# An encoder kernel with 64 sets of matmuls that nobody reads, set between the last norm and the output

## The chip, the cores and the metric

The kernel runs on one core of one Trainium2 chip. The metric is the device time of one execution in microseconds, taken on the chip. A profile is one execution recorded by the hardware profiler: its span goes from the first instruction to the end of the last one, and the engines in it are TensorE (PE, with its weight loads shown apart as PEld), VectorE (DVE), ScalarE (ACT), GpSimd (POOL) and SyncE (SP, which issues the DMAs here).

## The reference

A two-layer bidirectional encoder on 256 tokens of width 2048, all in float32. Each layer norms its input, projects it, runs a differential attention and a latent attention, merges the two through gates, adds the result to x, adds a SwiGLU and adds a gated embedding. At the end stands a norm:

```python
def rmsnorm(x, g, eps=NORM_EPS):
    xf = x.astype(jnp.float32)
    y = xf * lax.rsqrt(jnp.mean(xf * xf, axis=-1, keepdims=True) + eps)
    return (y * g.astype(jnp.float32)).astype(x.dtype)
...
        x = x + sigmoid(rmsnorm(x, g_ple[i]) @ w_ple_gate[i]) * e
    return rmsnorm(x, g_final)
```

## The kernel before

Everything is kept transposed: 128 channels on the partitions, 256 tokens along the row, 16 such blocks for the width of 2048. `xT` is the residual, one tile of 16 blocks.

**Matmuls in two parts.** A float32 number is split into a high part, which is a copy in the type fp32r, and a low part, which is the rest. For weights, `piece` (L168 on) loads up to 1024 columns into `w`, lets ScalarE copy them into a tile of the tag `whi` (L181) and VectorE write the rest into one of the tag `wlo`. Each of these two tags has three buffers, so a new tile takes the place of the one made three pieces ago and waits until the matmuls that read it are done. Activations are split into `ua` and `ub`, 16 tiles each with the high part in columns 0 to 255 and the low part in columns 256 to 511.

**Three kinds of matmul in fp32r.** In `emit`, for a usual product, a high block of weights is the stationary operand and a whole row of 512 columns (both parts of an activation) moves past it (L211), then the low block with the 256 high columns (L212). If `whole` is set, as for the last block of the kernel, there are three matmuls of 256 columns each (L207, L208, L209). In `values` (L392 to L394) it is the other way round: a block of 128 tokens of `ua` is stationary, and 512 columns of weights move.

**Norms.** `norm` sums squares over the partitions with matmuls that have a block of 128 columns in plain float32 as stationary operand and one column of `ones` moving (L271); on the chip each plain float32 matmul is two records in the profile. `rsqrt` is a string of small VectorE instructions. `spread` puts the result onto all partitions, by two multiplications with the identity (`dg`) and one plain float32 matmul of 256 columns (L280).

**The end.** In the last loop, for the 16 output blocks of `w_pg`, ScalarE joins the two parts of the product (L236), takes a sigmoid (L695), squares the new `xT` block (L263, L260) and scales it by the final gain (L683). Behind the loop stand the last `norm` and `spread`, whose result R stays in a bank of PSUM of the pool `ps_at`, which has two banks, and six multiplications of `xT` by R, each followed by its DMA to the output (L704).

**Order.** The program is written with a scheduler that places instructions on the engines and puts in the waits; each engine then runs its own list in order. An instruction that overwrites something waits for those that read it earlier in the program.

Of the kernel before, what the change touches and what calls it, by code (L numbers as in the profile page):

```python
# [13 lines left out]
F32R = mybir.dt.float32r  # L14
I32 = mybir.dt.int32
AF = mybir.ActivationFunctionType
# [3 lines left out]
P = 128  # L20
T = 256
# [15 lines left out]
PT = 8  # L37
# [15 lines left out]
def encoder(ctx, tc, x, p, positions, cols, lams, wq, wk, wv, wcq, wckv, wkr, wga, wgb,  # L53
            w_q_up, w_kn, w_v, w_bd, w_bm, w_out, w_gate, w_up, w_down, w_pin, w_pg, rope_c, out):
    nc = tc.nc
    V, A, PE = nc.vector, nc.scalar, nc.tensor
# [3 lines left out]
    wts = pool("wts")  # L60
    tmp = pool("tmp")
    stat = pool("stat")
    ps_mm = pool("ps_mm", 4, space=PSUM)
# [3 lines left out]
    def scratch(tag, bufs, n=T):  # L67
        return tmp.tile([P, n], F32, tag=tag, name=tag, bufs=bufs)

    def bank(ps=ps_at, tag="at", name="at", shape=(P, 2 * T)):  # L70
        return ps.tile(list(shape), F32, tag=tag, name=name)

    def tt(o, a, b, op):
        return V.tensor_tensor(out=o, in0=a, in1=b, op=op)  # L74
# [4 lines left out]
    def ts(o, a, s1, s2, op0, op1=ALU.bypass):  # L79
        return V.tensor_scalar(out=o, in0=a, scalar1=s1, scalar2=s2, op0=op0, op1=op1)  # L80


    ua = [const.tile([P, 2 * T], F32R, name=f"ua{j}") for j in range(NC)]
# [12 lines left out]
    xT = const.tile([P, NC, T], F32, name="xT")  # L96
# [4 lines left out]
    at = 0  # L101
# [10 lines left out]
    ones = const.tile([P, P], F32, name="ones")  # L112
# [2 lines left out]
    aside = [fa(j) for j in range(5)]  # L115
    posi = aside[0][:, 0, :].bitcast(I32)
    posf = aside[0][:, 1, :]

    def tables():
        V.tensor_copy(posf, posi)  # L120
        got = []
        for i, name in enumerate("pm"):
            ang, k, r, a = (aside[j + i][:, m, :] for j in (1, 3) for m in range(2))
            ts(ang, posf, rc[:, 2 * i : 2 * i + 1], None, ALU.mult)
            ts(k, ang, 1.0 / TWO_PI, ROUND, ALU.mult, ALU.add)
            ts(k, k, ROUND, None, ALU.subtract)
            stt(r, k, -C1, ang, ALU.mult, ALU.add)
            stt(r, k, -C2, r, ALU.mult, ALU.add)
            stt(r, k, -C3, r, ALU.mult, ALU.add)
            ts(r, r, PI_IN, -PI_IN, ALU.min, ALU.max)  # L130
            stt(a, r, -1.0, r, ALU.mult, ALU.min)
            ts(a, a, math.pi / 2, None, ALU.add)
            cs = const.tile([P, T], F32, name="cos_" + name)
            sn = const.tile([P, T], F32, name="sin_" + name)
            A.activation(cs, a, AF.Sin)
            A.activation(sn, r, AF.Sin)
            ts(sn, sn, rc[:, 2 * i + 1 : 2 * i + 2], None, ALU.mult)
            got += [cs, sn]
        return got
# [74 lines left out]
    def product(src, us, whole=False):  # L214


        acc = bank(ps_mm, "mm", "mm")
        n = len(us)
        for a in range(0, n, PT):
            m = min(PT, n - a)  # L220
            hi, lo = piece(src[:, a * P : (a + m) * P], m)
            emit(acc, hi, lo, 0, us[a : a + m], a == 0, a + m == n, whole)
        return acc[:, :T] if whole else acc
# [10 lines left out]
    def joined(acc, o=None):  # L234
        t = scratch("join", 3)
        A.activation(t, acc[:, T:], AF.Copy)  # L236
        o = scratch("a", 4) if o is None else o
        tt(o, acc[:, :T], t, ALU.add)
        return o
# [7 lines left out]
    def rsqrt(src, n, eps, width):  # L247

        v, y, a = (stat.tile([P, 2 * DH], F32, tag="r" + s, name="r" + s, bufs=2)[:, :width] for s in "vya")
        ts(v, src, 1.0 / n, eps, ALU.mult, ALU.add)  # L250
        ts(y.bitcast(I32), v.bitcast(I32), -0.5, 1597463007.0, ALU.mult, ALU.add)
        for _ in range(3):
            stt(a, y, -0.5, y, ALU.mult, ALU.mult)
            tt(a, a, v, ALU.mult)
            stt(y, a, 1.5, y, ALU.add, ALU.mult)
        return y

    def square_into(acc, src, first):
        if first:
            A.activation(acc, src, AF.Square)  # L260
        else:
            sq = scratch("sq", 2)
            A.activation(sq, src, AF.Square)  # L263
            tt(acc, acc, sq, ALU.add)

    def norm(sums, n):

        s = bank()
        for j, a in enumerate(sums):
            for b in range(2):  # L270
                PE.matmul(s[:, b : b + 1], a[:, b * P : (b + 1) * P], ones[:, 0:1], start=j + b == 0, stop=j + b == len(sums))  # L271
        return rsqrt(s[:, 0:2], n, EPS, 2)

    def spread(col, copied=True):

        dg = stat.tile([P, 2, P], F32, tag="dg", name="dg", bufs=1)
        for b in range(2):
            ts(dg[:, b, :], ident, col[:, b : b + 1], None, ALU.mult)
        s = bank()
        PE.matmul(s[:, :T], ones, dg, start=True, stop=True)  # L280
        if not copied:
            return s[:, :T]
        row = stat.tile([P, T], F32, tag="row", name="row", bufs=2)
        A.activation(row, s[:, :T], AF.Copy)  # L284
        return row

    def normed(sums, one, two):

        got = [joined(one())]
        col = norm(sums, DM)  # L290
        got.append(joined(two()))
        return spread(col), col, got

    def squares():
        return stat.tile([P, T], F32, tag="ssq", name="ssq", bufs=2)

    def stream(us, gain):

        acc = squares()

        def add(c):
            split(us[c], xT[:, c, :], g(gain, c))
            square_into(acc, xT[:, c, :], c == 0)

        return acc, add
# [110 lines left out]
    for L in range(DEPTH):  # L416

        steps = values(wv[L], ua, None if L else load)
        for vd in steps:
            if L == 0 and vd is not None:  # L420
# [3 lines left out]
                with after_splits():  # L424
                    rcol = norm([sq0[0][:, j, :] for j in range(2)], DM)
                    next(steps)
                    R = spread(rcol)
                    cos_p, sin_p, cos_m, sin_m = tables()
                    lambdas()
                break  # L430
            if L:
                next(steps)
                rcol = norm([acc], DM)
                next(steps)
                R = spread(rcol)
                break
# [5 lines left out]
        for o, t in ((cr, cos_p), (sr, sin_p), (crm, cos_m), (srm, sin_m)):  # L442
            tt(o, t, R, ALU.mult)

# [17 lines left out]
        def latent(us, w, raws):  # L462
            ss = squares()
            for c in range(len(us)):
                tt(raws[c], joined(product(w[L, c], ua)), R, ALU.mult)
                square_into(ss, raws[c], c == 0)
# [55 lines left out]
        def gate(w, store, n):  # L522
            tt(store(n), joined(product(w[L, n], ua)), R, ALU.mult)

# [115 lines left out]
        acc, add = stream(ub, f"g_ffn{L}")  # L640
# [4 lines left out]

        R, _, pre = normed([acc], lambda: product(w_gate[L, 0], ub), lambda: product(w_up[L, 0], ub))
        pT, es = ua[14:], []
# [4 lines left out]
        for part, (f0, f1) in enumerate(FF_PARTS):  # L652
            for f in range(f0, f1):
                a = pre.pop(0) if pre else joined(product(w_gate[L, f], ub))
# [5 lines left out]
                b = pre.pop(0) if pre else joined(product(w_up[L, f], ub))  # L660
# [3 lines left out]
            if last:  # L664
                acc, add = stream(ub, f"g_ple{L}")
# [10 lines left out]
        R, _, pre = normed([acc], lambda: product(w_pg[L, 0], ub), lambda: product(w_pg[L, 1], ub))  # L676
        final = L == DEPTH - 1
        if final:
            sums = [squares(), squares()]
# [5 lines left out]
        else:  # L685
            acc, add = stream(ua, f"g_mix{L + 1}")
        for n in range(NC):
            if final and n == NC - 1:
                a = scratch("a", 4)
                tt(a, product(w_pg[L, n], ub, True), R, ALU.mult)  # L690
            else:
                a = pre.pop(0) if pre else joined(product(w_pg[L, n], ub))
# [5 lines left out]
            add(n)  # L698

    R = spread(norm(sums, DM), copied=False)  # L700
    for n, m in ((0, 1), (1, 1), (2, 2), (4, 4), (8, 4), (12, 4)):
        o = xT[:, n : n + m, :]
        tt(o, o, R[:, None, :].to_broadcast([P, m, T]), ALU.mult)
        nc.sync.dma_start(out[:, n : n + m, :], o)  # L704
# [84 lines left out]
```

## Time and profile before

| | us |
|---|---|
| Median of 2 runs | 2867.84 |
| The two runs | 2866.69 and 2868.99 |
| The profiled execution | 2867.58 |
| Its span | 2865.8 |

The 1.78 us between the profiled execution's time and its span lie outside the recorded instructions. On the page, a row of a group of instructions gives the line, the engine, the operation, what is written and read (`out<-in`, moving operand first for a matmul), the shape and the count, then the busy time in us and the mean length of one in ns. A row of the timeline gives the start in us, the length in us, the engine, the line, the operation and how many were merged, and in brackets how long the engine had been idle and what ended that. Matmul lengths overlap: the time from one start to the next is what a matmul costs in a stream.

### The profile page before, as it was taken

The page shows a single profiled execution, that of the slowest core. Times are in us where ns is not written, and L with a number is a line of the kernel's source. Part 1 is how long each engine was busy: PE and PEld are TensorE (multiplying, and loading weights), DVE is VectorE, ACT ScalarE, POOL GpSimd, SP SyncE. Part 2 cuts the span into 40 slices and gives each one's busy share as a digit, 9 for nine tenths or more (in the row PEclk, how much of TensorE's full clock was granted, in tenths as well). Part 3 has the DMA queues.
Part 4 walks back from the last instruction along what each step waited for, and adds up shares of the span by engine and source line. Part 5 has one row for each costly group of instructions (what it writes and reads, how often), then busy time and mean ns, then how long its engine had stood idle before and what let it go on. Part 6 is the DMA issues. An engine that isn't in the chain of part 4 may idle for free.

```text
span 2865.8 us, 43980 instructions
## 1 busy us (share of the span) xinstructions
PE 2845.8 (99%) x16750; PEld 2507.7 (88%) x16750; DVE 2063.3 (72%) x3529; ACT 1524.2 (53%) x2529; POOL 1.7 (0%) x9
## 2 busy tenths in 40 slices
PE   9999999999999999999999999999999999999998
PEld 7888888888888888888888888888888888888887
DVE  7898658776666666677859976687766666666776
ACT  6676555554444444455646755555544444444554
POOL 0000000000000000000000000000000000000000
PEclk9999999999999999999999999999999999999999
DMA  7544566555665566566655445566556656655654
GB/s 233 171 162 148 162 193 199 192 191 187 184 199 194 182 198 201 194 193 191 189 188 166 154 154 168 193 197 194 188 188 185 198 194 187 200 194 194 193 190 140
DMA packets 156019, 532.40 MB, mean 186 GB/s; under 512 B 16928, under 2 KB 23840, under 8 KB 155808
## 3 DMA queue, kind: packets, MB, share of 16 engines
q1 hardware_dynamic: 155376, 529.01, 58.1%
q8 instruction: 131, 2.15, 0.3%
q14 instruction: 80, 0.66, 0.1%
q10 hardware_dynamic: 432, 0.59, 0.1%
HBM read 527.43 MB, written 2.10 MB: 185 GB/s over the span
## 4 chain that ended last, share of the span: by engine, by line
PE 98%; DVE 1%; ACT 0%; DMA 0%; issue 0%; SPq 0%; DVEq 0%
PE mm L211 61%; PE mm L212 31%; PE S L341 1%; PE mmv L394 1%; PE mmv L393 1%; PE mmv L392 1%; PE at L359 0%; PE at L563 0%; PE at L620 0%; DMA w<-in_wv 0%; DVE wlo L74 0%; DVE a L74 0%; PE at L280 0%; DVE xT L74 0%; ACT E L350 0%
## 5 line engine op out<-in xcount | busy, mean ns | idle before, releaser
L181 ACT ACTIVATE whi<-w 128x1024 fp32r<-128x1024 f32 (+2 forms) x1029 | 1067.0, 1037 | 1267.6 <-issue 722.6
L74 DVE TENSOR_TENSOR wlo<-w,whi 128x1024 fp32r<-128x1024 f32 (+2 forms) x1029 | 1229.6, 1195 | 703.8 <-ACT whi L181 694.7
L211 PE MATMUL mm<-ub,whi 128*128 128x512 f32 x3952 | 1360.8, 392 | 0.0
L211 PE MATMUL mm<-ua,whi 128*128 128x512 f32 x3744 | 1283.4, 390 | 0.0
L212 PE MATMUL mm<-ub,wlo 128*128 128x256 f32 x3952 | 1096.8, 278 | 0.0
L212 PE MATMUL mm<-ua,wlo 128*128 128x256 f32 x3744 | 1036.3, 277 | 0.0
L211 PEld LDWEIGHTS mm<-ub,whi 128*128 128x128 f32 x3952 | 741.9, 188 | 158.7
L211 PEld LDWEIGHTS mm<-ua,whi 128*128 128x128 f32 x3744 | 702.1, 188 | 143.9
L212 PEld LDWEIGHTS mm<-ub,wlo 128*128 128x128 f32 x3952 | 741.8, 188 | 0.8
L212 PEld LDWEIGHTS mm<-ua,wlo 128*128 128x128 f32 x3744 | 702.9, 188 | 2.3 <-DVE wlo L74 0.6
L74 DVE TENSOR_TENSOR a<-mm,join 128x256 f32<-128x256 f32 x421 | 175.7, 419 | 0.3 <-ACT join L236 0.2
L236 ACT ACTIVATE join<-mm 128x256 f32<-128x256 f32 x453 | 166.8, 369 | 5.0 <-PE mm L212 4.8
L74 DVE TENSOR_TENSOR xT<-xT,mm 128x256 f32<-128x256 f32 x256 | 106.9, 420 | 41.5 <-PE mm L212 37.7
L74 DVE TENSOR_TENSOR a<-a,row 128x256 f32<-128x256 f32 x207 | 87.4, 424 | 6.6 <-ACT row L284 0.8
L392 PE MATMUL mmv<-whi,ua 128*128 128x512 f32 x128 | 50.5, 396 | 3.8 <-ACT whi L181 3.8
L74 DVE TENSOR_TENSOR a<-a 128x256 f32<-128x256 f32 x120 | 51.0, 425 | 4.0
L74 DVE TENSOR_TENSOR ua<-a,ua 128x256 fp32r<-128x256 f32 x120 | 50.2, 418 | 1.0 <-ACT ua L244 1.0
L393 PE MATMUL mmv<-whi,ua 128*128 128x512 f32 x128 | 50.6, 396 | 0.0
L244 ACT ACTIVATE ua<-a 128x256 fp32r<-128x256 f32 x120 | 48.4, 403 | 2.7 <-DVE a L74 2.6
L350 ACT ACTIVATE E<-S,nm 128x256 f32<-128x256 f32 x96 | 44.3, 472 | 5.1 <-DVE nm L80 5.1
L394 PE MATMUL mmv<-wlo,ua 128*128 128x512 f32 x128 | 46.8, 397 | 0.1
L74 DVE TENSOR_TENSOR ssq<-ssq,sq 128x256 f32<-128x256 f32 x97 | 40.7, 420 | 0.5 <-ACT sq L263 0.5
(154 smaller groups left out, 1161.7 us busy)
## 6 DMA issues: line engine op xcount, KB each, us to landing
w<-in_w_gate SPq DMA_DIRECT2D x176, 512.0 KB, 4.7
w<-in_w_up SPq DMA_DIRECT2D x176, 512.0 KB, 4.7
w<-in_w_down SPq DMA_DIRECT2D x128, 512.0 KB, 4.2
w<-in_wga SPq DMA_DIRECT2D x64, 512.0 KB, 3.8
w<-in_wgb SPq DMA_DIRECT2D x64, 512.0 KB, 4.4
w<-in_w_out SPq DMA_DIRECT2D x64, 512.0 KB, 4.4
w<-in_w_pg SPq DMA_DIRECT2D x64, 512.0 KB, 4.7
w<-in_w_down SPq DMA_DIRECT2D x64, 384.0 KB, 3.7
```

Source lines behind the costliest of these rows:

```text
L74: return V.tensor_tensor(out=o, in0=a, in1=b, op=op)
L181: last_split[:] = A.activation(hi[:, :m], w[:, :m], AF.Copy), tt(lo[:, :m], w[:, :m], hi[:, :m].bitcast(F32), ALU.subtract)
L211: PE.matmul(acc, hi[:, s], u, start=start, stop=False)
L212: PE.matmul(acc[:, T:], lo[:, s], u[:, :T], start=False, stop=stop)
L236: A.activation(t, acc[:, T:], AF.Copy)
L244: return A.activation(hi, src, AF.Copy), tt(lo, src, hi.bitcast(F32), ALU.subtract)
L341: PE.matmul(S[:, b, :], q[:, b * P : (b + 1) * P], k, start=j == 0, stop=j == len(pairs) - 1)
L350: last_exp[0] = A.activation(E[:, b, :], S[:, b, :], AF.Exp, bias=nm[:, b : b + 1], scale=scale, accum_out=sm[:, b : b + 1])
L392: PE.matmul(banks[b], xh, hi[:, s], start=a + j == 0, stop=False)
L393: PE.matmul(banks[b], xl, hi[:, s], start=False, stop=False)
L394: last_mm[:] = [PE.matmul(banks[b], xh, lo[:, s], start=False, stop=a + j == n - 1)]
```

## The change

A function `others` is called between the last `spread` and the six multiplications. It copies the first four blocks of `xT` into one tile of the tag `whi` and one of the tag `wlo` (here named `side`), and then runs 64 sets of matmuls, all held in the order of the program:

- 32 sets of the values' kind: two banks, with three blocks j each; for each block and bank three matmuls of 512 columns, `ua` stationary and `sh`, `sh`, `sl` moving. That is 18 matmuls a set.
- 32 sets of rows of 256 columns: one bank, seven blocks j, with `sh` stationary and the high part of `ua` moving, then `sl` stationary and the low part of `ua` moving. That is 14 matmuls a set.
- Ahead of each set stands either `quarters` (five matmuls of 256 columns, `sl` stationary) or `sums` (four plain float32 matmuls with a block of `xT` stationary and one column moving, as in `norm`), by turns, in a bank of `ps_at`.
- The start of the slice in `sh` is 16, 32, 48 or 0 columns, and that in `sl` 0, 16, 32 or 48, in all 16 combinations.

Nothing reads the banks that these matmuls write. The six multiplications, which come later in the program, overwrite `xT`, which `sums` reads.

```diff
+    def others():
+        src = xT[:, :4, :].rearrange("p c t -> p (c t)")
+        sh = wts.tile([P, PT * P], F32R, tag="whi", name="side", bufs=3)
+        sl = wts.tile([P, PT * P], F32R, tag="wlo", name="side", bufs=3)
+        for t in (sh, sl):
+            A.activation(t, src, AF.Copy)
+        keep = tc.keep_in_program_order
+        mm = lambda *a, **k: keep(PE.matmul(*a, **k))
+
+        def quarters(at):
+            for j in range(5):
+                mm(at[:, :T], sl[:, j * P : (j + 1) * P], ua[j][:, :T], start=j == 0, stop=j == 4)
+
+        def sums(at):
+            for j in range(4):
+                mm(at[:, j : j + 1], xT[:, j, :P], ones[:, 0:1], start=True, stop=True)
+
+        for h in range(4):
+            for l in range(4):
+                oh, ol = 16 * ((h + 1) % 4), 16 * l
+                for first in (quarters, sums):
+                    first(bank(name="between"))
+                    accs = [bank(ps_mm, "mm", "t" + chr(97 + h) + chr(97 + l)) for _ in range(2)]
+                    for j in range(3):
+                        for b in range(2):
+                            xh, xl = ua[j][:, b * P : (b + 1) * P], ua[j][:, T + b * P : T + (b + 1) * P]
+                            mm(accs[b], xh, sh[:, oh : oh + 2 * T], start=j == 0, stop=False)
+                            mm(accs[b], xl, sh[:, oh : oh + 2 * T], start=False, stop=False)
+                            mm(accs[b], xh, sl[:, ol : ol + 2 * T], start=False, stop=j == 2)
+        for h in range(4):
+            for l in range(4):
+                oh, ol = 16 * ((h + 1) % 4), 16 * l
+                for first in (quarters, sums):
+                    first(bank(name="between"))
+                    acc = bank(ps_mm, "mm", "c" + chr(97 + h) + chr(97 + l))
+                    for j in range(7):
+                        mm(acc[:, :T], sh[:, oh + j * P : oh + (j + 1) * P], ua[j][:, :T], start=j == 0, stop=False)
+                        mm(acc[:, :T], sl[:, ol + j * P : ol + (j + 1) * P], ua[j][:, T:], start=False, stop=j == 6)
...
     R = spread(norm(sums, DM), copied=False)
+    others()
     for n, m in ((0, 1), (1, 1), (2, 2), (4, 4), (8, 4), (12, 4)):
         o = xT[:, n : n + m, :]
         tt(o, o, R[:, None, :].to_broadcast([P, m, T]), ALU.mult)
```

In the built program the lists of VectorE, GpSimd and SyncE are those of before. TensorE's list has the 1312 new matmuls at its very end, behind the matmul of `spread` at L280. ScalarE's list has the two copies near its end: the first just ahead of the `join` of the last block but one (14), the second just behind it.

## The prediction

> **What bounds the kernel now.** First the page, for its busy times and its chain of waits.
>
> ```profile
> span 2865.8 us, 43980 instructions
> PE 2845.8 (99%) x16750; PEld 2507.7 (88%) x16750; DVE 2063.3 (72%) x3529; ACT 1524.2 (53%) x2529; POOL 1.7 (0%) x9
> PE 98%; DVE 1%; ACT 0%; DMA 0%; issue 0%; SPq 0%; DVEq 0%
> ```
>
> TensorE is busy for 99% of the span and carries 98% of the chain that ended last. All its idle time together is 2865.8 - 2845.8 = 20 us, so long matmul work that is added cannot vanish into gaps. What it costs depends on how fast such matmuls follow each other, and on how the end of the kernel hangs together. So next the timeline of the last 16 us, where the new work is put.
>
> ```profile
> 2849.87 0.28 PE L209 MATMUL mm<-ub,wlo 128*128 128x256 f32 x1
> ...
> 2852.48 0.61 PE L271 MATMUL at<-ones,ssq 128*128 128x1 f32 x4 [1.99 <-ACT ssq L260]
> ...
> 2855.82 1.22 PE L280 MATMUL at<-dg,ones 128*128 128x256 f32 x2 [2.74 <-DVE dg L80]
> 2857.08 4.74 DVE L74 TENSOR_TENSOR xT<-xT,at 128x256 f32<-128x256 f32 x6 [1.31 <-PE at L280]
> 2857.53 4.65 SPq L704 DMA_DIRECT2D out_y<-xT  x6
> ```
>
> The last product ends, the norm goes through four engines, L280 ends at 2855.82 + 1.22 = 2857.04, and 0.04 later VectorE begins the six multiplications. From their start to the end of the span are 2865.8 - 2857.08 = 8.7 us, multiplications and output DMAs, in which TensorE has nothing to do.
>
> **Where the new matmuls lie.** They stand behind L280 in TensorE's list, and all that they read is there by then, so they start as it ends. The six multiplications do not run beside them: they overwrite `xT`, which every `sums` reads, the last one included. That one stands ahead of the last set of 14 matmuls. So the whole string but these 14 is pushed in between L280 and the multiplications; the 8.7 us after it stay as they are, and only the 14 are hidden under them.
>
> **The price of a matmul of 512 columns and of a `sums`.** `values` has the same form as the first 32 sets: a block of `ua` stationary, 512 columns of weights moving. And once a norm is put into its stream:
>
> ```profile
> 44.83 0.40 PE L394 MATMUL mmv<-wlo,ua 128*128 128x512 f32 x1
> 45.06 0.39 PE L392 MATMUL mmv<-whi,ua 128*128 128x512 f32 x1
> 45.29 0.40 PE L393 MATMUL mmv<-whi,ua 128*128 128x512 f32 x1
> 45.53 0.40 PE L394 MATMUL mmv<-wlo,ua 128*128 128x512 f32 x1
> 45.77 0.40 PE L392 MATMUL mmv<-whi,ua 128*128 128x512 f32 x1
> 46.00 0.40 PE L393 MATMUL mmv<-whi,ua 128*128 128x512 f32 x1
> 46.23 0.95 PE L271 MATMUL at<-ones,fb 128*128 128x1 f32 x8
> 47.05 0.48 PE L394 MATMUL mmv<-wlo,ua 128*128 128x512 f32 x1
> 47.36 0.40 PE L392 MATMUL mmv<-whi,ua 128*128 128x512 f32 x1
> ```
>
> A length of 0.40 is not the price, since the next one starts earlier: five steps from 44.83 to 46.00 are 1.17 us, 0.234 each. From 46.00 to 47.36 are 1.36 us for two such matmuls and eight plain float32 records; less 2 x 0.234, the eight cost 0.89. Eight records are four matmuls, just what one `sums` issues, and the changes to and from fp32r are in it.
>
> 32 sets x 18 = 576 matmuls x 0.234 = 134.8 us. 32 `sums` x 0.89 = 28.5 us.
>
> **The price of a matmul of 256 columns.** The last product runs with `whole`: weights stationary, 256 columns of an activation moving, as in the second 32 sets and in `quarters`. There are 16 each of L207, L208 and L209:
>
> ```profile
> L209 PE MATMUL mm<-ub,wlo 128*128 128x256 f32 x16 | 4.5, 282 | 0.0
> L208 PE MATMUL mm<-ub,whi 128*128 128x256 f32 x16 | 4.5, 281 | 0.0
> L207 PE MATMUL mm<-ub,whi 128*128 128x256 f32 x16 | 4.5, 279 | 0.0
> ```
>
> ```profile
> 2844.33 0.28 PE L207 MATMUL mm<-ub,whi 128*128 128x256 f32 x1
> ```
>
> The first of the 48 starts at 2844.33 and the last, shown above, at 2849.87: 5.54 us in 47 steps, 0.118 each. 32 sets x 14 and 32 `quarters` x 5 are 608 matmuls x 0.118 = 71.7 us. The string is 134.8 + 28.5 + 71.7 = 235.0 us.
>
> **What comes off.** The last 14 matmuls are hidden: 14 x 0.118 = 1.65. The first multiplication needs only the first block of `xT`, so it can start after the first of the four matmuls of the last `sums`; the next ones need the second and then the fourth, 0.22 us a matmul against 0.42 for a multiplication, so three quarters of that `sums`, 0.67, are hidden too. 235.0 - 2.3 = 232.7.
>
> **The clock at the start of the string.** The norm at the end leaves TensorE mostly idle, and the granted clock falls:
>
> ```profile
> 2854.00:2854.50 0.50, 0.00 (x0) 0.00 (x0) 0.40 (x4) 0.00 (x0) 0.00 (x0) 1.00 0.00 0
> 2854.50:2855.00 0.50, 0.00 (x0) 0.00 (x0) 0.43 (x3) 0.00 (x0) 0.00 (x0) 0.59 0.00 0
> 2857.00:2857.50 0.50, 0.04 (x1) 0.00 (x0) 0.42 (x2) 0.00 (x0) 0.00 (x0) 0.50 0.00 0
> ```
>
> ```profile
> 99.82 0.59 PE L280 MATMUL at<-dg,ones 128*128 128x256 f32 x2
> ```
>
> In these windows the third number from the right is the granted clock: 1.00, then 0.59, then 0.50 when L280 ends. L280 shows it: two records take 1.22 us here and 0.59 at 99.82. So the string starts at half speed. For how long, the start of the kernel tells:
>
> ```profile
> 1.05 3.67 PE L407 MATMUL at<-ones 128*128 128x128 f32 x16 [1.05 <-DVE ones L113]
> 4.87 0.50 PE L392 MATMUL mmv<-whi,ua 128*128 128x512 f32 x1 [0.15 <-ACT whi L181]
> 5.20 0.39 PE L393 MATMUL mmv<-whi,ua 128*128 128x512 f32 x1
> 5.43 0.40 PE L392 MATMUL mmv<-whi,ua 128*128 128x512 f32 x1
> ```
>
> The first 512-column matmul takes 0.33 to the next, the second 0.23, so full speed came at about 5.0, some 3.9 us after TensorE's first matmul. The same from 2855.82 gives 2859.7, which is 2.7 us into the string; half of that, 1.4 us, is lost. If the clock comes back at once, nothing is lost; if it takes twice as long, 3.3. The Trainium skill, TensorE: Matmul & The Clock Gate, section "Part 1: The HAM clock gate", speaks against any string set behind such an idle stretch: the gate watches free-running windows of about 3.4 us, halves the clock after an idle one and gives it back after a busy one. By that page alone the loss is some 1.7 us in place of 1.4, and the sum 0.3 higher; the fall to 0.50 agrees with it.
>
> **ScalarE's two copies.** A copy of 128x1024 takes 1.06 us, and two of them stand in its list where the last blocks are finished.
>
> ```profile
> 2841.61 1.06 ACT L181 ACTIVATE whi<-w 128x1024 fp32r<-128x1024 f32 x1 [0.62 <-PE mm L211]
> 2844.53 0.39 ACT L236 ACTIVATE join<-mm 128x256 f32<-128x256 f32 x1 [1.55 <-PE mm L212]
> ...
> 2847.68 0.43 DVE L74 TENSOR_TENSOR ssq<-ssq,sq 128x256 f32<-128x256 f32 x1 [0.48 <-ACT sq L263]
> 2850.18 0.42 DVE L74 TENSOR_TENSOR a<-mm,row 128x256 f32<-128x256 f32 x1 [2.08 <-PE mm L209]
> ```
>
> The first takes the buffer of a piece that block 14 uses, so it waits for block 14's last matmul, as the `join` behind it does; it pushes the `join` by about 1.06, and the second pushes the squares of block 13 behind it by as much again. Queued behind them is the finish of blocks 13 and 14: joins, sigmoid, squares, scalings on ScalarE and the sums on VectorE. Followed through, the last of these on VectorE ends at about 2849.7 instead of 2848.11; VectorE then had 2.08 us of idle time until TensorE ended block 15 at about 2850.15. So it costs nothing, by a margin of 0.4 us; with the cover gone it would cost at most 2 x 1.06 = 2.1.
>
> **The sum.** 232.7 + 1.4 = 234.1 us. Against the profiled execution: 2867.58 + 234.1 = 3101.7, with a span of 2865.8 + 234.1 = 3099.9. The median lies 0.26 above the profiled execution, so 3102 on its basis. That is 8.2% slower; less than 2% is about what a measurement of this kernel cannot tell from no change.
>
> **What the trace does not show: the places.** No matmul of before starts 16, 32 or 48 columns into a block. How much a price can hang on something other than the shape, the usual pair of L211 and L212 shows:
>
> ```profile
> 86.13 0.39 PE L211 MATMUL mm<-ua,whi 128*128 128x512 f32 x1
> 87.83 0.39 PE L211 MATMUL mm<-ua,whi 128*128 128x512 f32 x1
> ```
>
> ```profile
> 2835.23 0.40 PE L211 MATMUL mm<-ub,whi 128*128 128x512 f32 x1
> 2835.58 0.40 PE L211 MATMUL mm<-ub,whi 128*128 128x512 f32 x1
> 2835.93 0.40 PE L211 MATMUL mm<-ub,whi 128*128 128x512 f32 x1
> ```
>
> Five pairs in 1.70 us are 0.340 a pair; near the end of the kernel a pair takes 0.350. The prices above, 0.234 + 0.118 = 0.352, are those of the slower pair. With the faster one, 3% come off 206.5 us of fp32r matmuls: -6 us. From above the nearest row is a weight load that is not hidden at all:
>
> ```profile
> L211 PEld LDWEIGHTS mm<-ub,whi 128*128 128x128 f32 x3952 | 741.9, 188 | 158.7
> ```
>
> That would be 0.19 on a matmul, and on all 1184 of them 223 us. I take nothing for the places, because three arrangements of the operands (L211 with L212, `values`, `whole`) lie within 3% of each other, and keep a part of the upper bound for the range.
>
> **The rivals.**
>
> *Bad places (0.12).* At some starts the load of the next weights and the moving row get in each other's way, and the load is no longer hidden. If one combination in eight is so, 148 matmuls x 0.19 = 28 us: 3130. For it speaks that the pair has two speeds in one kernel; against it that the two differ by 0.010, not by 0.19.
>
> *Good places (0.10).* The string runs at the faster pair's speed: 3096. The Trainium skill, the same page, section "Back-to-back issue gap", would go further, with columns over 2.4 GHz and 2.5 ns whatever the place: 0.216 and 0.109, an estimate of 16 us less and 3086. No row here goes so low (the best pair takes 0.340, and these two make 0.325), so I give that 0.02 of the 0.10.
>
> *A stop at each set (0.05).* Each of the 64 first matmuls waits for a semaphore of TensorE itself, for the previous user of its bank. If that empties the pipeline, the load of 0.19 and the time from the next start to the result, 0.28 - 0.12 = 0.16, come on top: 64 x 0.35 = 22 us, 3124. Against it: the matmul waited for is 14 or 18 matmuls back, over 1.6 us, and long done.
>
> *The other side (0.01).* The matmuls' results are read by nobody; if the build leaves them out, only the two copies stay, under cover, and the time is 2868. The point that decides is the count of TensorE's records, 16750 or about 18190 (1184 and 2 x 128 more). Against it: the built list has them all. Were they only to fill idle time, they would have 20 us of it and need 235.
>
> **How the numbers follow.** My forecast, 3102, has 0.72; its own range is 3094 to 3111, from the faster pair to the slow clock for twice as long with a cover that fails. The range of 3093 to 3118 takes in that and nearly all of the good places, and the milder half of the bad ones, and leaves out about 0.16. All cases but the last are slower by more than 2%, which is 2925: slower 0.99, same 0.01, faster 0.
>
> **What would show it.** In the changed kernel's profile: TensorE's records up by about 1440 and its busy time by about 234; the six multiplications at about 3091, released by TensorE; steps of 0.23 in the first 32 sets, 0.118 in the second, 0.9 for a `sums`; half the granted clock for some 3 us from 2857; VectorE's last sum of squares of block 14 before 2850.2. It is wrong if the steps hang on the places by more than a few per cent, if gaps show ahead of each set, or if the multiplications start early.

## The result, and the profile after

| | us |
|---|---|
| Before, median | 2867.84 |
| With the change, median | 3099.51 (3099.12 and 3099.89) |
| Ratio | 1.081, 95% interval 1.0793 to 1.0828 |
| Span of the profiled execution | 3097.3, before 2865.8 |

The change makes the kernel 231.7 us slower; 3102 was forecast. First the page of the changed kernel, in the lines that answer to those of before.

```profile
span 3097.3 us, 46863 instructions
PE 3080.4 (99%) x18190; PEld 2718.3 (88%) x18190; DVE 2063.3 (67%) x3529; ACT 1524.7 (49%) x2531; POOL 1.7 (0%) x9
```

TensorE has 1440 more records, 2 x 128 + 1184, and is busy for 234.6 us more. VectorE's count and busy time are those of before, and ScalarE has the two copies more. Then the timeline of the changed kernel from the last product on (start, length, engine, line).

```profile
2849.24 0.28 PE L251 MATMUL mm<-ub,wlo 128*128 128x256 f32 x1
...
2849.56 0.42 DVE L74 TENSOR_TENSOR a<-mm,row 128x256 f32<-128x256 f32 x1 [1.02 <-PE mm L251]
...
2855.19 1.22 PE L322 MATMUL at<-dg,ones 128*128 128x256 f32 x2 [2.74 <-DVE dg L80]
2855.85 1.63 PE L129 MATMUL between<-ua,side 128*128 128x256 f32 x5
2857.28 4.66 PE L129 MATMUL taa<-side,ua 128*128 128x512 f32 x18
2861.78 0.94 PE L129 MATMUL between<-ones,xT 128*128 128x1 f32 x8
2862.59 4.39 PE L129 MATMUL taa<-side,ua 128*128 128x512 f32 x18
2866.81 0.76 PE L129 MATMUL between<-ua,side 128*128 128x256 f32 x5
2867.41 4.34 PE L129 MATMUL tab<-side,ua 128*128 128x512 f32 x18
...
3086.66 1.81 PE L129 MATMUL cdd<-ua,side 128*128 128x256 f32 x14
3088.31 0.95 PE L129 MATMUL between<-ones,xT 128*128 128x1 f32 x8
3088.63 4.75 DVE L74 TENSOR_TENSOR xT<-xT,at 128x256 f32<-128x256 f32 x6 [233.49 <-PE between L129]
3089.07 4.66 SPq L747 DMA_DIRECT2D out_y<-xT  x6
3089.12 1.89 PE L129 MATMUL cdd<-ua,side 128*128 128x256 f32 x14
```

L129 is the helper that records every added matmul, L251 is what was L209, and L322 what was L280. The string follows L322 without a gap. The six multiplications wait 233.49 us, released by a `between` that reads `xT`, the last `sums`. The rest of that `sums` and the last 14 matmuls run beside them, and from the multiplications' start to the end of the span are 3097.3 - 3088.63 = 8.7 us, as before.

The prices are differences of starts. A set of 18 with 512 columns and a `quarters` behind it: 2866.81 - 2862.59 = 4.22, with 0.09 of the `sums` ahead in it; a set that a `quarters` precedes, 2871.59 - 2867.41 = 4.18 (the `sums` behind `tab` starts at 2871.59), is 0.232 a matmul. The 15 such sets at full clock take 4.12 to 4.22. A set of 14 with 256 columns: 3088.31 - 3086.66 = 1.65, 0.118 each. A `quarters` at full clock: 2867.41 - 2866.81 = 0.60. A `sums`: 2862.59 - 2861.78 = 0.81, and the first matmul behind it is 0.09 late, so 0.90.

At the head of the string the same things are dearer. The first `quarters` takes 2857.28 - 2855.85 = 1.43 and the first set 4.50. The granted clock of the changed kernel (third number from the right, in slices of 0.5 us; the first number behind the comma is TensorE's busy time) tells why:

```profile
2854.50:2855.00 0.50, 0.00 (x0) 0.00 (x0) 0.46 (x3) 0.00 (x0) 0.00 (x0) 0.65 0.00 0
2858.00:2858.50 0.50, 0.50 (x3) 0.38 (x3) 0.00 (x0) 0.00 (x0) 0.00 (x0) 0.94 0.00 0
```

A slice at 0.65 has 0.70 of its time at 0.50, so the clock fell at 2854.65; the last slice has 0.06 x 2 x 0.5 = 0.06 us at 0.50, so it came back at 2858.06, 3.41 us later. The string lost half of the stretch from 2855.85 on, 1.1 us.

### The profile page after: what moved, and what is told of

Its sections match the earlier page's. It is cut to its first block, busy times and chain, and to the rows that moved or that the text cites. A ratio compares the mean times of both kernels' runs of the same rounds, so it can differ in the third digit from the quotient of the medians.

```text
span 3097.3 us, 46863 instructions
## 1 busy us (share of the span) xinstructions
PE 3080.4 (99%) x18190; PEld 2718.3 (88%) x18190; DVE 2063.3 (67%) x3529; ACT 1524.7 (49%) x2531; POOL 1.7 (0%) x9
## 4 chain that ended last, share of the span: by engine, by line
PE 98%; DVE 1%; ACT 0%; DMA 0%; issue 0%; SPq 0%; DVEq 0%
PE mm L253 56%; PE mm L254 28%; PE between L129 1%; PE S L383 1%; PE mmv L436 1%; PE mmv L435 1%; PE mmv L434 1%; PE at L401 0%; PE at L605 0%; PE at L662 0%; PE taa L129 0%; PE tda L129 0%; PE tac L129 0%; PE tdd L129 0%; PE tcc L129 0%; PE tab L129 0%
```

## The experiments

Times are medians; the kernel before, run beside them, had medians of 2866.73 to 2867.66.

**What holds the multiplications.** `sums` reads the tile of ones in place of `xT`.

```diff
-                mm(at[:, j : j + 1], xT[:, j, :P], ones[:, 0:1], start=True, stop=True)
+                mm(at[:, j : j + 1], ones, ones[:, 0:1], start=True, stop=True)
```

> The stationary operand of each sums is the tile of ones in place of a block of xT, so nothing in the string reads xT; all matmul counts and shapes stay. Theory (the string lies in between because the multiplications overwrite xT): they are released by the spread matmul at about 2856.4 and end, with their DMAs, long before TensorE does. The span then ends with TensorE's last matmul, at about 3091 plus about 1 us: 5 to 6 us less than with the change, about 3094. Rival (they are held by the bank of R or by their place in the program): they still start at about 3088.6 and the time stays at 3099.5.

Measured: 3094.75, ratio 1.0792 (1.0776 to 1.0808), 4.8 less than with the change. The timeline of this kernel:

```profile
2858.22 1.63 PE L129 MATMUL between<-ua,side 128*128 128x256 f32 x5
...
2858.82 4.74 DVE L74 TENSOR_TENSOR xT<-xT,at 128x256 f32<-128x256 f32 x6 [1.32 <-PE at L322]
...
3091.34 1.89 PE L129 MATMUL cdd<-ua,side 128*128 128x256 f32 x14
```

The multiplications now start beside the string, at its first matmuls, and the span (3094.1) ends 0.9 us after TensorE's last matmul, at 3091.34 + 1.89. So it was the overwriting of `xT` that put the whole string in the way of the output. Freed of that, the string still costs its full length: nothing but TensorE itself is waited for. In this execution the string starts 2.4 us later, at 2858.22; counted from the string's start to the end of the span, the kernel is 5.6 us shorter (3094.1 - 2858.22 = 235.9 against 3097.3 - 2855.85 = 241.4).

**The clock, first try.** The string stands between `norm` and `spread`.

```diff
-    R = spread(norm(sums, DM), copied=False)
+    col = norm(sums, DM)
     others()
+    R = spread(col, copied=False)
```

> The string stands between norm and spread, right behind the last sum over the partitions, so TensorE goes into it with less than 2.5 us of idle time. Theory (the string's first matmuls are slow because the clock falls after the idle stretch): the granted clock stays at 1.00, the first quarters takes 0.59 in place of 1.43 us, and the spread matmul behind the string takes 0.59 in place of 1.22. In sum 2.7 us of small VectorE work come under cover, 1.2 and 0.6 are saved, 2.3 us that were hidden behind the start of the multiplications are not any more: about 2 us less than with the change, 3097. Rival (the slow start is a first use of new operands or a fetch of code): the first quarters takes 1.4 us again and the time is 3098.5 or more.

Measured: 3098.94 (1.0807, 1.0789 to 1.0825), no clear difference from the change. My expectation failed, and so did the rival as I put it: the first `quarters` takes 2853.12 - 2852.44 = 0.68, not 1.4. The head of the string and the granted clock of this kernel:

```profile
2852.44 0.84 PE L129 MATMUL between<-ua,side 128*128 128x256 f32 x5
2853.12 5.89 PE L129 MATMUL taa<-side,ua 128*128 128x512 f32 x18
```

```profile
2853.00:2853.50 0.50, 0.50 (x5) 0.46 (x4) 0.41 (x3) 0.00 (x0) 0.00 (x0) 0.84 0.00 0
2856.50:2857.00 0.50, 0.50 (x4) 0.37 (x3) 0.00 (x0) 0.00 (x0) 0.00 (x0) 0.75 0.00 0
```

The clock fell at 2853.34, 0.9 us into the string, with TensorE busy, and came back at 2856.75, again 3.41 us later. So the whole stretch lay in the string and cost 1.7 us, not 1.1. The fall seems to answer to what was before it: the norm leaves TensorE idle from 2849.98 to 2851.97 in this kernel. That fits what the Trainium skill says (TensorE: Matmul & The Clock Gate, "Part 1: The HAM clock gate"): the gate watches free-running windows of about 3.4 us, 3413 ns by that page. The page speaks of an idle window; here TensorE was busy for 1.42 of the 3.41 us before the fall, so a partly idle one was enough. The matmul of `spread`, now behind the string, took 0.59 in place of 1.22, as expected.

**The clock, second try.** Four of the `quarters` stand ahead of the norm, so that its first gap is filled too, and the other work of the string again between `norm` and `spread`.

```diff
+        for _ in range(4):
+            quarters(bank(name="between"))
+        yield
...
-                    first(bank(name="between"))
+                    if h or first is sums:
+                        first(bank(name="between"))
...
-    R = spread(norm(sums, DM), copied=False)
-    others()
+    string = others()
+    next(string)
+    col = norm(sums, DM)
+    next(string, None)
+    R = spread(col, copied=False)
```

(The second change is in the values' kind alone, for its first four sets with a `quarters`.)

> Four of the quarters stand ahead of the last norm and the rest of the string between norm and spread, so TensorE has hardly any idle time before the string. The run with the string between norm and spread alone had the clock fall to 0.50 at 2853.3, inside the string, for 3.41 us. Theory (the clock is decided by how idle TensorE was in a window of 3.41 us that runs freely): with the gaps filled it stays at 1.00, the string has no slow part (1.6 us less) and the gap of 2.1 us in the norm is used: about 3095. Rival (any wait for the norm lets it fall, or it falls after plain float32 matmuls): a stretch of 0.50 again and 3097 or more.

Measured: 3096.66 (1.0798, 1.0780 to 1.0816). The timeline and the clock of this kernel:

```profile
2851.07 0.28 PE L255 MATMUL mm<-ub,wlo 128*128 128x256 f32 x1
2851.19 2.56 PE L129 MATMUL between<-ua,side 128*128 128x256 f32 x20
2853.59 0.95 PE L317 MATMUL at<-ones,ssq 128*128 128x1 f32 x8
2854.40 4.37 PE L129 MATMUL taa<-side,ua 128*128 128x512 f32 x18
...
3086.35 4.74 DVE L74 TENSOR_TENSOR xT<-xT,at 128x256 f32<-128x256 f32 x6 [229.13 <-PE at L326]
```

```profile
2851.00:2853.00 2.00, 2.00 (x20) 2.00 (x19) 1.09 (x3) 0.42 (x1) 0.00 (x0) 1.00 0.00 0
2853.00:2855.00 2.00, 2.00 (x18) 1.91 (x17) 0.54 (x4) 0.93 (x2) 0.00 (x0) 1.00 0.00 0
2855.00:2858.00 3.00, 3.00 (x15) 2.46 (x14) 1.91 (x11) 0.00 (x0) 0.00 (x0) 1.00 0.01 3
```

With the gaps filled the clock stays at 1.00, and the row of the first set is 4.37 long in place of 4.66. From the last matmul of the product to the first multiplication are 3086.35 - 2851.07 = 235.3 us, 4.1 less than with the change (3088.63 - 2849.24 = 239.4). The span is only 2.2 less, since the same code ahead of the string ended 1.8 us later in this execution. The theory holds: it is the idle time inside the norm that halves the clock.

**The places.** All slices at column 0 (first diff and expectation), and at odd columns (second).

```diff
-                oh, ol = 16 * ((h + 1) % 4), 16 * l
+                oh, ol = 0, 0
```

```diff
-                oh, ol = 16 * ((h + 1) % 4), 16 * l
+                oh, ol = (1, 3, 5, 7)[h], (1, 2, 4, 7)[l]
```

> All slices start at column 0; counts and shapes stay. Theory (the place hardly matters): the 512-column steps stay at 0.231 to 0.234, the 256-column steps at 0.116 to 0.120, and the time at 3099.5 within 3. Rival (the shifted places are dearer): up to 6 us less, 3093.5, with steps of 0.227 and 0.114 as in the faster pair.

> The slices start at columns 1, 3, 5, 7 in one tile and 1, 2, 4, 7 in the other, so 4 to 28 bytes off in place of 0 to 192; counts and shapes stay. Theory (the place hardly matters): the same steps and 3099.5 within 4. [...]

Measured: 3101.69 (1.0817, 1.0800 to 1.0833) and 3101.38 (1.0814, 1.0798 to 1.0831). Both medians are some 2 us above the change, but the intervals overlap with its 1.0793 to 1.0828, so the traces have to tell what the place does. The timeline and the clock of the kernel with all slices at 0:

```profile
2858.00 1.63 PE L129 MATMUL between<-ua,side 128*128 128x256 f32 x5
...
2865.60 4.46 PE L129 MATMUL taa<-side,ua 128*128 128x512 f32 x18
...
3093.23 1.88 PE L129 MATMUL cdd<-ua,side 128*128 128x256 f32 x14
```

```profile
2855.00:2855.50 0.50, 0.00 (x0) 0.00 (x0) 0.40 (x4) 0.00 (x0) 0.00 (x0) 0.67 0.00 0
2861.50:2862.00 0.50, 0.50 (x3) 0.34 (x2) 0.00 (x0) 0.00 (x0) 0.00 (x0) 0.51 0.00 0
```

Here the clock was at 0.50 from 2855.17 to 2861.99, 6.82 us, twice 3.41, of which 4.0 lie in the string: 2.0 us lost in place of 1.1. With odd columns the clock was at 0.50 for as long. The length does not come from the place: with shorter rows and with fp32r `sums`, at the places of the change, the clock is also down for twice 3.41. The place's own part is read from the second `taa` to the last `cdd`, at full clock: 3093.23 - 2865.60 = 227.63, against 3089.12 - 2862.59 = 226.53 with the change. With odd columns, it is 3090.19 - 2862.27 = 227.92:

```profile
2862.27 4.52 PE L129 MATMUL taa<-side,ua 128*128 128x512 f32 x18
...
3090.19 1.90 PE L129 MATMUL cdd<-ua,side 128*128 128x256 f32 x14
```

In the first two experiments, with the places of the change, the same stretch is 226.39 and 226.52. So 1.1 and 1.4 us, or 0.5 and 0.6%, hang on the place: column 0 is not the cheap place, and odd starts are none of the bad places of the prediction. The rest of what separates these profiled executions from that of the change is the clock and the start of the string, at 2858.00 and 2854.72 in place of 2855.85; how the medians divide is not shown.

**The columns.** The first 32 sets with 320, 384, 448 and 512 columns.

```diff
+                            n = 320 + 64 * (l % 4) if l < 3 else 512
-                            mm(accs[b], xh, sh[:, oh : oh + 2 * T], start=j == 0, stop=False)
+                            mm(accs[b][:, :n], xh, sh[:, oh : oh + n], start=j == 0, stop=False)
...
```

> In the first 32 sets the moving rows have 320, 384, 448 and 512 columns (by the inner place) in place of 512; the counts stay. Theory (the step is the columns that stream, and the load is hidden): 512 columns in 0.232 are 0.453 ns a column, so steps of 0.145, 0.174, 0.203 and 0.232; 144 matmuls x (192 + 128 + 64) columns x 0.453 ns are 25 us less, 3074.5. Rival (a floor of each matmul, such as the 0.188 of a weight load as the profile shows it, sets the step): the short rows stop at about 0.19 and the time falls by under 17 us.

Measured: 3075.76 (1.0726, 1.0705 to 1.0748). The timeline of this kernel:

```profile
2865.70 3.29 PE L129 MATMUL tab<-side,ua 128*128 128x384 f32 x18
2868.83 0.95 PE L129 MATMUL between<-ones,xT 128*128 128x1 f32 x8
...
2873.44 3.83 PE L129 MATMUL tac<-side,ua 128*128 128x448 f32 x18
2877.11 0.95 PE L129 MATMUL between<-ones,xT 128*128 128x1 f32 x8
...
2891.99 2.77 PE L129 MATMUL tba<-side,ua 128*128 128x320 f32 x18
2894.59 0.95 PE L129 MATMUL between<-ones,xT 128*128 128x1 f32 x8
```

That is 23.8 less than with the change, where 25 was expected. Steps of 3.13 / 18 = 0.174, 3.67 / 18 = 0.204 and 2.60 / 18 = 0.144, as the columns say. The floor of the rival does not exist: 0.19 is the length of a weight load in the profile, not its price. What is missing from the 25 fits the clock: it came back at 2860.62, 4.5 us into this string, which lost 2.2 us in place of 1.1.

**Plain float32 or fp32r.** The `sums` with fp32r operands, two columns moving.

```diff
-                mm(at[:, j : j + 1], xT[:, j, :P], ones[:, 0:1], start=True, stop=True)
+                mm(at[:, 2 * j : 2 * j + 2], sh[:, j * P : (j + 1) * P], ua[j][:, 0:2], start=True, stop=True)
```

> Each sums takes fp32r operands (blocks of sh stationary, two columns of ua moving) in place of plain float32; the counts of matmuls stay. Theory (a plain float32 matmul is two passes, each with its own weight load of 0.112): half the records, 0.45 us in place of 0.90 for a sums, 32 x 0.45 = 14.4 us less, 3085. Rival (the price is that of a change of type or of the pipeline running empty around such short matmuls): 3095 or more.

Measured: 3081.67 (1.0747, 1.0725 to 1.0768), 17.8 less than with the change, not 14.4. I had missed that this edit also frees the multiplications, as nothing reads `xT` any more. The timeline of this kernel:

```profile
2873.32 0.50 PE L129 MATMUL between<-ua,side 128*128 128x2 f32 x4
2873.69 4.42 PE L129 MATMUL tab<-side,ua 128*128 128x512 f32 x18
```

Four records, 0.37 from start to start in place of 0.81: 32 x 0.44 = 14.1. With the 5.6 of the first experiment that is 19.7; the clock takes back 1.6, since it came back 5.5 us into this string (2862.04 - 2856.54), and 18.1 are left. So the price goes with the records: eight in 0.81 are 0.10 each, four in 0.37 are 0.09. This edit also takes away the change between the kinds of number, so alone it does not clear that rival; the next kernel does.

**A wait on the matmul just before.** A second `sums` behind each `quarters` or `sums`, in the same bank.

```diff
                     first(bank(name="between"))
+                    sums(bank(name="between"))
```

> Behind each quarters or sums stands another sums, in the same bank of PSUM, so its first matmul waits for the matmul just before it and not for one 14 or 18 back. It adds 64 sums at 0.90, 57.6 us. Theory (a wait costs only if what it waits for is still under way): each of the 64 new waits stops the stream for about 0.35 us (0.19 load, 0.16 to the result), 22 us, so 3099.5 + 57.6 + 22 = 3179. Rival (TensorE's waits on itself cost nothing, since its matmuls end in order): 3157.

Measured: 3178.35 (1.1084, 1.1062 to 1.1106), 78.8 more than with the change. The timeline of this kernel and, below it, its clock late in the string:

```profile
2873.17 0.75 PE L129 MATMUL between<-ua,side 128*128 128x256 f32 x5
2873.98 1.05 PE L129 MATMUL between<-ones,xT 128*128 128x1 f32 x8
2874.90 4.41 PE L129 MATMUL tab<-side,ua 128*128 128x512 f32 x18
2879.15 2.06 PE L129 MATMUL between<-ones,xT 128*128 128x1 f32 x16
2881.07 4.42 PE L129 MATMUL tab<-side,ua 128*128 128x512 f32 x18
```

```profile
3118.50:3121.00 2.50, 2.50 (x14) 2.50 (x14) 0.00 (x0) 0.00 (x0) 0.00 (x0) 0.50 0.00 0
```

The `quarters` takes 0.81 to the next start in place of 0.60: such a stop costs 0.21 here, not 0.35. Two `sums` in a row take 2881.07 - 2879.15 = 1.92 where one takes 0.81: the second costs 1.11, again 0.90 and 0.21. No kind of number changes between the two, so the bulk of the 0.90 is not the price of such a change.

57.6 for the `sums` and 64 x 0.21 = 13.4 make 71.0. Of the other 7.8 us, 4.8 are clock: the first stretch at 0.50 lasted to 2865.51, 8.4 us into this string, which lost 4.2 in place of 1.1, and the clock fell a second time in mid-string, from 3118.10 to 3121.51, which cost 1.7. The rest is about what the 32 `sums` behind a `quarters` take beyond the 0.81 to the next start, 2874.90 - 2873.98 = 0.92. So the total agreed with my 22 us by luck, and the rival (no cost) falls by the step itself. What matters for the prediction is the other side of it: a wait on a matmul 14 or 18 back showed no stop at all, 0.118 x 5 = 0.59 for a `quarters` that has one.

**The kernel before with the gaps filled.** The lesson of the clock, tried where it might help.

```diff
+    def filler(n):
+        at = bank(name="filler")
+        for j in range(n):
+            tc.keep_in_program_order(PE.matmul(at[:, :T], ua[j % 8][:, :P], ua[j % 8][:, :T], start=j == 0, stop=j == n - 1))
+
-    R = spread(norm(sums, DM), copied=False)
+    filler(18)
+    col = norm(sums, DM)
+    filler(20)
+    R = spread(col, copied=False)
```

> The kernel before, with 18 unread matmuls of 256 columns ahead of the last norm and 20 between norm and spread, each 0.118, which is 2.1 and 2.4 us for the two gaps of 2.0 and 2.7 us. Theory (the clock falls because of these gaps, and the spread matmul pays for it): the granted clock stays at 1.00 up to the spread matmul, whose two records take 0.59 in place of 1.22 us, and the way from the last product to the first multiplication is 0.5 us shorter, 6.4 in place of 6.9; the time is 2867.3, no difference that can be measured. Rival (the spread matmul is slow for the wait before it, not for the clock, or the fillers are in its way): 1.22 again, and the same way or up to 1 us more.

Measured: 2866.99 against 2866.73 beside it, ratio 1.0001 (0.9992 to 1.0010): no difference, as expected. The timeline of this kernel shows the small gain that the time cannot:

```profile
2848.19 0.28 PE L209 MATMUL mm<-ub,wlo 128*128 128x256 f32 x1
...
2854.24 0.67 PE L280 MATMUL at<-dg,ones 128*128 128x256 f32 x2 [0.33 <-DVE dg L80]
2854.95 4.74 DVE L74 TENSOR_TENSOR xT<-xT,at 128x256 f32<-128x256 f32 x6 [0.85 <-PE at L280]
```

L280 takes 0.67 in place of 1.22, and from the last product matmul to the multiplications are 6.76 us in place of 7.21.

## Why the prediction was right

The mechanism and the sum held: 3102 forecast, 3099.5 measured, inside the range. Step by step:

- *Where the string lies.* Right: behind L322, with the multiplications behind its last `sums` and 14 matmuls under their cover. The first experiment showed the reason by taking it away.
- *512 columns at 0.234.* 0.232: 576 of them make it about 1.2 us less.
- *256 columns at 0.118.* Right, in the sets and in `quarters`.
- *A `sums` at 0.89.* 0.90. The multiplications began 0.32 us into the last one (3088.63 - 3088.31), where the prediction has one matmul of four, 0.22.
- *The clock.* Right in kind, 1.1 lost in place of 1.4, but that the size came so near is luck: over the kernels tried here the string lost 0 to 4.2. The length of 3.9 us was misread. The first 512-column matmul of the kernel before takes 0.33 to the next, but the one behind the norm takes 0.31 too (47.05 to 47.36), and there the granted clock is 1.00. So the step of 0.33 does not show half speed. The granted clock reads 1.00 in every slice of the kernel's first 6 us, though L407's 16 records, 0.42 us at the median and 0.30 at the shortest, speak for a slow stretch: L359's of the same shape take 0.27 at the median. The runs show stretches of 3.41 us or a multiple.
- *ScalarE's copies.* Right, they cost nothing. VectorE still had 1.02 us of idle time ahead of the last block, where 2.08 had been; I had foreseen 0.4.
- *The end before the string.* L322 ended at 2856.41 in this execution, L280 at 2857.04 before: 0.6 us that is no part of the change. And the string did not start as L322 ended, as forecast: its first row starts at 2855.85, 0.56 before that. With the 1.2 and the 0.3 these make 2.7; the forecast was too high by 2.4.
- *The range.* Its upper end, 3111, does not follow from what it names: the slow clock for twice as long, 1.9, and a failed cover, 2.1, make 3106.
- *The rivals.* Bad places: not found, at multiples of 16 columns or at odd ones; places are worth about 1 us. Good places: the matmuls stayed at the price of `values` and `whole`. A stop at each set: none; a `quarters` behind a set takes 0.60, the price of its five matmuls. The string left out: 1440 records more.

What makes the usual pair take 0.340 in one stretch and 0.350 in another was not tried and stays open.

## What to carry to other kernels

On a kernel whose slowest engine is busy for 99%, added work on it is priced by the steps between starts in rows of the same form, not by the lengths of the rows, and it came out within 1%. Ask of added work not only how long it takes but what reads and overwrites its operands: a read of `xT` held the whole output back, which cost some 5 us more than the work itself (4.8 by the medians). Short waits in a norm can halve TensorE's clock for what follows, and only filling them, not moving the work closer, kept it.

## What the runs showed of the hardware

The granted clock changes in steps of one length. It was at 0.50 for 3.41 us with the change, in the first experiment and with the string ahead of `spread`; for twice that with all slices at 0, at odd columns, with shorter rows and with fp32r `sums`; and for three times that, 10.24, at the head of the string with a second `sums`. The time at 1.00 fits the same step: with the change, from 2858.06 to the next fall at 3093.58, are 235.52 us, 69 x 3.413. How many steps the slow stretch takes, and how much of it lies in the string, decided what the string lost: 1.1 to 4.2 us.

In two kernels the head of the string is the same up to the first `sums`, but it lies at another place in the step. The first 3.41 us behind the fall, with the change and with fp32r `sums`:

```profile
2854.65:2858.06 3.41, 2.87 (x9) 2.57 (x10) 0.48 (x2) 0.00 (x0) 0.00 (x0) 0.50 0.00 0
2855.22:2858.63 3.41, 2.75 (x9) 2.48 (x10) 2.06 (x7) 0.00 (x0) 0.00 (x0) 0.50 0.05 17
```

With TensorE busy for 2.87 us the clock came back at the end, and with 2.75 it stayed down for another 3.41. Where the bound lies was not tried.

The clock can also fall in the middle of the string: in the kernel with three times as many one-column matmuls it fell at 3118.10, with TensorE busy for 3.35 of the 3.41 us before. Matmuls of one column keep the row of the profile full, but, it seems, do not count in full for the clock; this was not tried by itself.
